# Value products of seven attention heads, one matmul per key block over all queries behind it

## Chip, cores and metric

The kernel runs on one core of one Trainium2 chip. The metric is the device time of one execution in microseconds (us); lower is better. PE is TensorE (PEld its weight loads), DVE is VectorE, ACT is ScalarE, POOL is GpSimd, SP is the engine whose queue issues the loads.

## The reference

One layer of a decoder with 512 tokens and width 1024 in float32. The part that matters here is the attention: two causal mixers with eight heads each, whose outputs are gated and added.

```python
def nsa_mixer(q, kc, vc, ks, vs, kw, vw, gates):
    ...
        s = jnp.einsum('bqgrd,bngd->bgrqn', qb, kc) * scale
        p_cmp = masked_softmax(s, cmp_end[None, :] <= t[:, None])
        o_cmp = jnp.einsum('bgrqn,bngd->bqgrd', p_cmp.astype(vc.dtype), vc)
    ...
        o_slc = jnp.einsum('bgrqkl,bgqkld->bqgrd', p.astype(vs.dtype), v_sel)
    ...
        o_win = jnp.einsum('bgrqk,bkgd->bqgrd', p.astype(vw.dtype), v_w)
        o = gb[..., 0:1] * o_cmp + gb[..., 1:2] * o_slc + gb[..., 2:3] * o_win
def mla_mixer(q, k, v):
    ...
        p = masked_softmax(s, kpos[None, :] <= t[:, None])
        o = jnp.einsum('bhqk,bkhd->bqhd', p.astype(v.dtype), v)
```

With 512 tokens the selected and the window branch both see all keys up to the query, so each is plain causal attention, as the MLA mixer is. What is computed here is, for each head and branch, O = P V with a causal P of 512 queries by 512 keys.

## The kernel before

**Stages.** Norm, adaLN and the first projections (to about 70 us in the trace), key/value group 0 of the NSA mixer together with the compression MLP (to 136 us), the heads (to 545 us), output projection (to 600 us) and the FFN. A matmul on float32 data is made in three: each operand is split into a rounded high part and a low rest (`split`, lines 82 to 84: ACT makes the high part, DVE the rest), and `mm3` (lines 91 to 94) issues high x high, high x low, low x high into one PSUM group.

**Weights.** `load_w` (lines 99 to 116) takes a raw tile `wr` from a pool of five (`raw_unit`, line 97), loads 128 x 512 floats into it from SP's queue, and splits it into `wh` and `wl` (four tiles of each). The raw tile is free when DVE has made `wl`. The same pool serves the adaLN products (`gemv`, lines 124 to 128) and, in `kv_group`, the two rope tables (lines 241 to 244), which stay in their raw tiles until `rope_2x2` (lines 207 to 216) has run for both token halves. In the stage to 136 us a round of the group's `gemm256` (lines 186 to 200) splits one tile of key or value weights for 24 matmuls of 256 columns and then lets the compression take four tiles, each for four matmuls of 256 columns.

**Heads.** `half` (lines 734 to 786) does 256 queries of one head and branch: scores, softmax, transposes of the probabilities by PE, `split` into `PTh` and `PTl`, and then the value products in `pv` (lines 721 to 732). The probabilities' transposes lie key block by key block, each for the queries that see it. Half 0 has queries 0 to 255 and key blocks 0 and 1, half 1 has queries 256 to 511 and key blocks 0 to 3. So the products are `mm3` groups of

```python
                if j <= a:
                    o, r = O[:, c0:c0 + 256], slice(j * 256, (j + 1) * 256)
                else:
                    o, r = O[:, c0 + P:c0 + 256], slice((a + 1) * 256, (a + 1) * 256 + P)
                mm3(o, vh, vl, PTh[:, r], PTl[:, r], first and j == 0, j == a + 1)
```

256 columns, and of 128 for the last key block of the half. An NSA head has two such branches (`nsa_half`, lines 814 to 827) and the compressed one (`cmp_lane`, lines 788 to 812); an MLA head has one (`mla_half`). Heads 0 to 6 go through `nsa_head` and `mla_head` (lines 838 to 849), head 7 is written out by halves.

**Order.** The tile framework's scheduler makes the order on each engine at build time, from priorities and from which tiles are free; each engine then runs its list in order. `pv` has a raised priority. So a change in a pool's size or in one helper moves instructions elsewhere.

Of the kernel before, what the change touches and what calls it, by code (L numbers as in the profile page):

```python
# [10 lines left out]
F32 = mybir.dt.float32  # L11
F32R = mybir.dt.float32r
# [5 lines left out]
P = 128  # L18
# [20 lines left out]
def tile_hybrid_layer(  # L39
# [56 lines left out]
    def raw_unit():  # L96
        return wp.tile([P, 512], F32, name="wr", tag="wr", bufs=5)
# [39 lines left out]
    # ---------------------------------------------------------------- constants  # L137
# [38 lines left out]
    krp = const.tile([P, NT, 2, RD], F32, name="krp")  # L176
# [8 lines left out]
    # ================================================================ heads  # L185
# [181 lines left out]
    def mla_kv(h):  # L367
# [26 lines left out]
        vec.tensor_mul(kraw, kraw, rk.unsqueeze(2).to_broadcast([P, NT, HD]))  # L394
        vec.tensor_tensor(krp, krr.unsqueeze(2).to_broadcast([P, NT, 2, RD]),
# [12 lines left out]
    # ================================================================ phase 1  # L408
    with tc.tile_pool(name="p1", bufs=1) as p1:
# [126 lines left out]
        # ---- cq and the branch gates  # L536
# [17 lines left out]
        # ---- second group: ckv, kr, vc of the second group  # L554
# [12 lines left out]
        # ---- compressed branch inputs, features on partitions  # L567
# [16 lines left out]
        # ---- ckv, kr  # L584
# [31 lines left out]
        # gains and constants of the heads  # L616
# [8 lines left out]
        # ---- compression  # L625
# [79 lines left out]
    # ================================================================ attention  # L705
# [3 lines left out]
    with tc.tile_pool(name="p2", bufs=1) as p2:  # L709
# [24 lines left out]
        def half(hf, qk, V, nrq, gate, O, first, sc=None):  # L734
# [37 lines left out]
            blocks = []  # L772
            for j in range(a + 2):
                for x2 in range(2):
                    if j <= a + x2:
                        blocks.append(off[x2] + j * P)
            PTh = p2.tile([P, 896], F32R, name="PTh", tag="PTh", bufs=2)
            PTl = p2.tile([P, 896], F32R, name="PTl", tag="PTl", bufs=2)
            for b0 in range(0, len(blocks), 4):
                bl = blocks[b0:b0 + 4]  # L780
                tr = bank("T")
                for e, o in enumerate(bl):
                    pe.transpose(tr[:, e * P:(e + 1) * P], Pt[:, o:o + P], ident)  # L783
                cs = slice(b0 * P, (b0 + len(bl)) * P)
                split(PTh[:, cs], PTl[:, cs], tr[:, 0:len(bl) * P])
            pv(O, first, hf, (PTh, PTl), V)

        def cmp_lane(h, sc, O, i0, i1):
# [20 lines left out]
            pt = p2.tile([P, 896], F32R, name="pt", tag="PTh", bufs=2)[0:96, 0:n * P]  # L809
# [4 lines left out]
        def nsa_half(h, hf, O, sc):  # L814
            qh, ql, _, nrq = NQ[h]
            Kt, V = KV[h // 4]
            for br in range(2):
                kh, kl = Kt[br]

                def vf(j, br=br):  # L820
                    s = slice((j % 2) * 256 + br * P, (j % 2) * 256 + (br + 1) * P)
                    return V[j // 2][0][:, s], V[j // 2][1][:, s]
                qf = [lambda ts, q=q: q[:, ts] for q in (qh, ql)]
                half(hf, [(qf[0], kh), (qf[0], kl), (qf[1], kh)], vf, nrq, gates[:, 3 * h + 1 + br, :], O, hf == 0 and br == 0,
                     None if br else sc)
                if not br and (hf or h == 7):
                    cmp_lane(h, sc, O, 2 * hf if h == 7 else 0, 2 * hf + 2)

        def mla_half(h, hf, O):
# [5 lines left out]
            half(hf, [(qn[0], knh), (qn[0], knl), (qn[1], knh), (qr[0], krh), (qr[1], krl[0:RD])],  # L835
                 lambda j: (vh[:, j * P:(j + 1) * P], vl[:, j * P:(j + 1) * P]), nrq[:, h % 2, :], None, O, hf == 0)

        def nsa_head(h):
            O = bank("O")
            sc = sm.tile([P, NT, 32], F32, name="sc", tag="sc", bufs=1)  # L840
            nsa_half(h, 0, O, sc)
            nsa_half(h, 1, O, sc)
            return O

        def mla_head(h):
            O = bank("O")
            mla_half(h, 0, O)
            mla_half(h, 1, O)
            return O
# [22 lines left out]
        for h in range(7):  # L872
# [11 lines left out]
            if h < 6:  # L884
                acc = p2.tile([P, 512], F32, name="acc2", tag="acc2")
                if h < 4:
                    c0, dst = ((3 * D, fS), (4 * D, fA))[h // 2]
                    c0 += (h % 2) * 512
                    gemv(acc, c0, True)
                    gemv_cols(acc, c0, dst[:, 4 * (h % 2):4 * (h % 2) + 4], h >= 2)  # L890
                else:
                    gate_acc(acc, 2 * D, h - 4)
                    gate_out(ga, acc, h - 4)
# [13 lines left out]
    # ================================================================ output projection and FFN  # L907
# [214 lines left out]
```

## Time and profile before

| | us |
|---|---|
| median of 3 runs | 950.85 |
| lowest, highest | 950.5, 951.32 |
| span of the profiled execution | 947.3 |
| PE matmul busy | 914.3 |
| DVE busy | 690.8 |
| ACT busy | 511.0 |

The span is the time between the first and the last instruction in the profile; the runs' times hold about 3.5 us more, for what lies around it (the profiled execution has no time of its own beside its span). Busy PE is a modelled figure, since matmuls overlap: a matmul's own duration says little, the step from one start to the next is its price. In the tables a line of `kernel.py` is L and its number; L87 is the one line that issues all of `mm`'s matmuls, so they are told apart by their operands (`psO<-PTh,Vh` is a value product of the NSA mixer, `psO<-PTh,vh` one of the MLA mixer).

### The profile page before, as it was taken

The page shows a single profiled execution, that of the slowest core. Times are in us where ns is not written, and L with a number is a line of the kernel's source. Part 1 is how long each engine was busy: PE and PEld are TensorE (multiplying, and loading weights), DVE is VectorE, ACT ScalarE, POOL GpSimd, SP SyncE. Part 2 cuts the span into 40 slices and gives each one's busy share as a digit, 9 for nine tenths or more (in the row PEclk, how much of TensorE's full clock was granted, in tenths as well). Part 3 has the DMA queues.
Part 4 walks back from the last instruction along what each step waited for, and adds up shares of the span by engine and source line. Part 5 has one row for each costly group of instructions (what it writes and reads, how often), then busy time and mean ns, then how long its engine had stood idle before and what let it go on. Part 6 is the DMA issues. An engine that isn't in the chain of part 4 may idle for free.

```text
span 947.3 us, 15181 instructions
## 1 busy us (share of the span) xinstructions
PE 914.3 (97%) x5271; PEld 801.2 (85%) x5271; DVE 690.8 (73%) x1513; ACT 511.0 (54%) x1241; POOL 51.1 (5%) x57
## 2 busy tenths in 40 slices
PE   3999899999999999999999999999999999999998
PEld 2899788889889998888889899988888888888886
DVE  6967979787977779688967788797787666622423
ACT  5556758566676557558766655445444444422221
POOL 1000101001000001001001010000000000000000
PEclk9999999999999999999999999999999999999999
DMA  9945682441331253341214265263363333333421
GB/s 298 341 112 145 180 232 82 134 136 35 115 87 34 57 170 101 101 128 43 56 46 134 75 189 150 76 175 107 95 183 101 93 97 100 94 96 101 143 91 44
DMA packets 135778, 113.06 MB, mean 119 GB/s; under 512 B 7514, under 2 KB 118678, under 8 KB 135702
## 3 DMA queue, kind: packets, MB, share of 16 engines
q1 hardware_dynamic: 134934, 110.00, 39.4%
q0 software_dynamic: 768, 2.11, 0.7%
q8 instruction: 41, 0.67, 0.3%
q14 instruction: 35, 0.29, 0.1%
HBM read 109.98 MB, written 2.10 MB: 118 GB/s over the span
## 4 chain that ended last, share of the span: by engine, by line
PE 87%; ACT 4%; DVE 4%; DMA 3%; issue 1%; SPq 0%; POOL 0%; DVEq 0%; ACTq 0%
PE psG L87 43%; PE psS L87 23%; PE psO L87 8%; PE psF L87 4%; PE psT L87 4%; PE psT L783 2%; DMA wr<-in_w_in_dram 1%; DVE wl L84 1%; ACT Pt L760 1%; DMA wr<-in_cmp_v_w_dram 1%; ACT wh L83 1%; DMA ada<-in_w_ada_dram 1%; DMA x<-in_x_dram 1%; ACT sq L223 1%; PE psT L808 0%
## 5 line engine op out<-in xcount | busy, mean ns | idle before, releaser
L83 ACT ACTIVATE wh<-wr 128x512 fp32r<-128x512 f32 (+3 forms) x304 | 186.7, 621 | 289.5 <-PE psS L87 95.0
L84 DVE TENSOR_TENSOR wl<-wr,wh 128x512 fp32r<-128x512 f32 (+3 forms) x304 | 203.6, 676 | 155.4 <-ACT wh L83 148.4
L87 PE MATMUL psG<-hTh,wh 128*128 128x512 f32 x192 | 76.5, 398 | 1.0 <-DVE qr L328 1.0
L87 PE MATMUL psG<-hTh,wl 128*128 128x512 f32 x192 | 76.3, 397 | 0.1
L87 PE MATMUL psG<-hTl,wh 128*128 128x512 f32 x192 | 76.3, 397 | 0.0
L87 PE MATMUL psS<-h2l,wh 128*128 128x512 f32 (+1 forms) x184 | 68.3, 371 | 0.0
L87 PE MATMUL psS<-h2h,wl 128*128 128x512 f32 (+1 forms) x184 | 68.2, 371 | 0.0
L87 PE MATMUL psG<-h2h,wh 128*128 128x512 f32 (+1 forms) x184 | 68.2, 372 | 0.0
L87 PE MATMUL psG<-h2h,wl 128*128 128x512 f32 (+1 forms) x184 | 68.2, 371 | 0.0
L87 PE MATMUL psG<-h2l,wh 128*128 128x512 f32 (+1 forms) x184 | 68.1, 371 | 0.0
L87 PE MATMUL psS<-h2h,wh 128*128 128x512 f32 (+1 forms) x184 | 68.0, 370 | 0.0
L760 ACT ACTIVATE Pt<-psS,nm 128x128 f32<-128x128 f32 (+2 forms) x96 | 51.1, 534 | 25.8 <-DVE nm L755 20.1
L83 ACT ACTIVATE PTh<-psT 128x384 fp32r<-128x384 f32 (+1 forms) x72 | 36.5, 528 | 22.4 <-PE psT L783 22.2
L84 DVE TENSOR_TENSOR PTl<-psT,PTh 128x384 fp32r<-128x384 f32 (+1 forms) x72 | 42.1, 597 | 8.7 <-ACT PTh L83 8.1
L122 DVE SCALAR_TENSOR_TENSOR acc<-wr,csil,acc 128x512 f32<-128x512 f32 x60 | 44.8, 747 | 2.7 <-DMA wr<-in_w_ada_dram 1.5
L87 PEld LDWEIGHTS psG<-hTh,wh 128*128 128x128 f32 x192 | 36.2, 188 | 7.6 <-PE psS L87 0.7
L87 PEld LDWEIGHTS psG<-hTh,wl 128*128 128x128 f32 x192 | 36.1, 188 | 7.1 <-DVE wl L84 0.5
L87 PEld LDWEIGHTS psG<-hTl,wh 128*128 128x128 f32 x192 | 36.1, 188 | 6.4
L87 PE MATMUL psG<-wh,hTh 128*128 128x256 f32 (+2 forms) x128 | 37.5, 303 | 2.5 <-ACT hTh L83 1.4
L87 PEld LDWEIGHTS psG<-h2h,wl 128*128 128x128 f32 x184 | 34.7, 189 | 6.0
L87 PEld LDWEIGHTS psS<-h2l,wh 128*128 128x128 f32 x184 | 34.7, 189 | 6.0
L87 PEld LDWEIGHTS psS<-h2h,wh 128*128 128x128 f32 x184 | 34.7, 188 | 6.0
(431 smaller groups left out, 2593.8 us busy)
## 6 DMA issues: line engine op xcount, KB each, us to landing
wr<-in_w_up_dram SPq DMA_DIRECT2D x88, 256.0 KB, 3.0
wr<-in_w_ada_dram SPq DMA_DIRECT2D x64, 256.0 KB, 2.9
wr<-in_w_in_dram SPq DMA_DIRECT2D x48, 256.0 KB, 3.0
wr<-in_w_down_dram SPq DMA_DIRECT2D x44, 256.0 KB, 2.6
ada<-in_w_ada_dram SPq DMA_DIRECT2D x32, 256.0 KB, 5.4
wr<-in_w_o_dram SPq DMA_DIRECT2D x32, 256.0 KB, 3.0
wr<-in_w_in_dram SPq DMA_DIRECT2D x32, 128.0 KB, 3.6
wr<-in_cmp_k_w_dram SPq DMA_DIRECT2D x16, 256.0 KB, 3.7
```

Source lines behind the costliest of these rows:

```text
L83: act.activation(hi, src, AF.Copy)
L84: vec.tensor_sub(lo, src, f(hi))
L87: ins = pe.matmul(o, lhsT, rhs, start=start, stop=stop, skip_group_check=True)
L122: vec.scalar_tensor_tensor(acc, w, csil[:, k:k + 1], acc, op0=ALU.mult, op1=ALU.add)
L223: act.activation(sq[:, 0:n], b, AF.Square, accum_out=dst)
L760: act.activation(Pt[:, off[x2]:off[x2] + nt[x2]], Sb[x2], AF.Exp, bias=nm[:, x2:x2 + 1], scale=-1.0, accum_out=sums[:, x2:x2 + 1])
L783: pe.transpose(tr[:, e * P:(e + 1) * P], Pt[:, o:o + P], ident)
```

## The change

For heads 0 to 6 the probabilities of both halves of a branch go into one pair of tiles, and `pv_head` issues the products when both are there: key block j meets all queries from block j on, in one `mm3` group of 512, 384, 256 and 128 columns. For key block 0 the columns lie in two pieces (0 to 255 and 640 to 895), which one access pattern reads. The tiles `PTh`, `PTl` and `pt` grow from 896 to 1280 columns, two of each as before. In turn the pool `wr` has four tiles in place of five, `krp` moves from a tile of its own into the tag `kr` (which `c2` of `comb_b` also uses), and `acc2` into a tile of the tag `U`. `cmp_lane` runs once per head for all four query blocks, as it did for these heads. Head 7 keeps its halves.

```diff
     def raw_unit():
-        return wp.tile([P, 512], F32, name="wr", tag="wr", bufs=5)
+        return wp.tile([P, 512], F32, name="wr", tag="wr", bufs=4)
...
-    krp = const.tile([P, NT, 2, RD], F32, name="krp")
...
+        krp = pj.tile([P, 512], F32, name="krp", tag="kr").rearrange("p (t a d) -> p t a d", t=NT, a=2)
...
+        HEAD_BLOCKS = (((0, 0), (0, 1), (1, 1)), ((1, 2), (1, 3), (0, 2), (0, 3), (2, 2), (2, 3), (3, 3)))
+        HEAD_AT = {1: (256, 384), 2: (896, 256), 3: (1152, 128)}
+
+        @priority(lambda: 100)
+        def pv_head(O, first, PT, V):
+            for j in range(NT):
+                vh, vl = V(j)
+                if j == 0:
+                    ph, pl = (bass.AP(tensor=t.tensor, offset=t.offset, ap=[t.ap[0], [640, 2], [1, 256]]) for t in PT)
+                else:
+                    at, n = HEAD_AT[j]
+                    ph, pl = (t[:, at:at + n] for t in PT)
+                mm3(O[:, j * P:S], vh, vl, ph, pl, first and j == 0, j == NT - 1)
...
-            PTh = p2.tile([P, 896], F32R, name="PTh", tag="PTh", bufs=2)
-            PTl = p2.tile([P, 896], F32R, name="PTl", tag="PTl", bufs=2)
+            if PT is None:
+                order = [(j, a + x2) for j in range(a + 2) for x2 in range(2) if j <= a + x2]
+                PTh = p2.tile([P, 1280], F32R, name="PTh", tag="PTh", bufs=2)
+                PTl = p2.tile([P, 1280], F32R, name="PTl", tag="PTl", bufs=2)
+                to = 0
+            else:
+                order = HEAD_BLOCKS[hf]
+                PTh, PTl = PT
+                to = hf * 384
...
+            if PT is not None:
+                return
             pv(O, first, hf, (PTh, PTl), V)
...
         def nsa_head(h):
             O = bank("O")
             sc = sm.tile([P, NT, 32], F32, name="sc", tag="sc", bufs=1)
-            nsa_half(h, 0, O, sc)
-            nsa_half(h, 1, O, sc)
+            for br in range(2):
+                args = nsa_args(h, br)
+                PT = pair_of_pt()
+                for hf in range(2):
+                    half(hf, *args, O, False, None if br else sc, PT)
+                pv_head(O, br == 0, PT, args[1])
+                if not br:
+                    cmp_lane(h, sc, O, 0, NT)
             return O
...
         def mla_head(h):
             O = bank("O")
-            mla_half(h, 0, O)
-            mla_half(h, 1, O)
+            PT = pair_of_pt()
+            for hf in range(2):
+                args = mla_args(h, hf)
+                half(hf, *args, O, False, None, PT)
+            pv_head(O, True, PT, args[1])
             return O
...
-                acc = p2.tile([P, 512], F32, name="acc2", tag="acc2")
+                acc = slot("U", "acc2")
```

PE, value products of half 0 of one NSA branch, before (`Vh` and `Vl` are the value block's high and low parts):

```order
L87 MATMUL psO<-PTh,Vh_1737 128x256
L87 MATMUL psO<-PTl,Vh_1737 128x256
L87 MATMUL psO<-PTh,Vl_1738 128x256
L87 MATMUL psO<-PTh,Vh_1737 128x128
L87 MATMUL psO<-PTl,Vh_1737 128x128
L87 MATMUL psO<-PTh,Vl_1738 128x128
```

Half 1 of the branch has, at another place of the list, nine more of 256 columns and three of 128.

PE, value products of a whole NSA branch, now, from its first matmul to its last:

```order
L87 MATMUL psO<-PTh,Vh_1736 128x512
...
L87 MATMUL psO<-PTl,Vh_1736 128x512
L87 MATMUL psO<-PTh,Vl_1737 128x512
L87 MATMUL psO<-PTh,Vh_1736 128x384
L87 MATMUL psO<-PTl,Vh_1736 128x384
L87 MATMUL psO<-PTh,Vl_1737 128x384
L87 MATMUL psO<-PTh,Vh_1740 128x256
L87 MATMUL psO<-PTl,Vh_1740 128x256
L87 MATMUL psO<-PTh,Vl_1741 128x256
L87 MATMUL psO<-PTh,Vh_1740 128x128
L87 MATMUL psO<-PTl,Vh_1740 128x128
L87 MATMUL psO<-PTh,Vl_1741 128x128
```

Eighteen matmuls in two places have become twelve in one; four projection matmuls stand where the line of dots is.

DVE, the rope of key group 0, first token half, before (`kg` is the key with its gain, the two rows with `wr` read the rope tables, each `wl` frees a weight's raw tile):

```order
L204 TENSOR_TENSOR kg<-psS,rowg 128x512
L84 TENSOR_TENSOR ckvTl_1053<-psF,ckvTh_1052 128x512
L208 TENSOR_TENSOR a_1389<-kg,wr 128x512
L84 TENSOR_TENSOR wl<-wr,wh 128x512
L211 TENSOR_TENSOR a_1390<-kg,wr 128x512
L84 TENSOR_TENSOR wl<-wr,wh 128x512
```

And now:

```order
L203 TENSOR_TENSOR kg<-psS,rowg 128x512
L84 TENSOR_TENSOR ckvTl_1052<-psF,ckvTh_1051 128x512
L207 TENSOR_TENSOR a_1388<-kg,wr 128x512
L210 TENSOR_TENSOR a_1389<-kg,wr 128x512
L84 TENSOR_TENSOR wl<-wr,wh 128x512
```

The reads of the tables have moved ahead of weight splits: from this `kg` to the last read of a table, for the second token half, five `wl` stood before and three stand now. SP's list of loads is the same in this stage in both.

## Rows read from the trace of the kernel before

**Rows 1.** The page's first part: busy us (share of the span) and instructions.
```profile
PE 914.3 (97%) x5271; PEld 801.2 (85%) x5271; DVE 690.8 (73%) x1513; ACT 511.0 (54%) x1241; POOL 51.1 (5%) x57
```

**Rows 2.** Busy time by stages, with the columns' names.
```profile
core 0: us, PE busy (x) PEld busy (x) DVE busy (x) ACT busy (x) POOL busy (x), PEclk, DMA share, GB/s
...
100.00:136.00 36.00, 32.36 (x235) 28.69 (x235) 30.87 (x58) 25.44 (x61) 5.27 (x3) 1.00 0.73 211
...
150.00:545.00 395.00, 387.70 (x2471) 344.85 (x2471) 318.49 (x832) 258.39 (x755) 31.67 (x29) 1.00 0.32 91
...
600.00:947.00 347.00, 342.95 (x1541) 284.90 (x1539) 209.27 (x314) 131.93 (x214) 0.55 (x1) 1.00 0.36 109
```

**Rows 3.** Waits, 100 to 136 us: us in total, times, longest.
```profile
SPq L112 <- DVE wl L84: 13.1, 11, 2.0
...
ACT wh L83 <- DMA wr<-in_cmp_v_w_dram: 3.0, 3, 2.0
PEld psG L87 <- DVE wl L84: 1.8, 3, 0.9
```

**Rows 4.** The chain in order of time: start, us, what.
```profile
148.94 1.56 PE psG L87 x9
...
542.44 18.64 PE psG L87 x155
...
653.86 5.44 PE psS L87 x24
```

**Rows 5.** Timeline of PE, value products: start, us, engine, line, operands.
```profile
266.61 0.33 PE L87 MATMUL psO<-PTh,Vh 128*128 128x256 f32 x1
266.78 0.28 PE L87 MATMUL psO<-PTl,Vh 128*128 128x256 f32 x1
...
267.30 0.44 PE L87 MATMUL psG<-hTh,wl 128*128 128x512 f32 x1
...
508.74 0.28 PE L87 MATMUL psO<-PTl,vh 128*128 128x256 f32 x1
...
509.69 0.22 PE L87 MATMUL psO<-PTh,vh 128*128 128x128 f32 x1
509.75 0.28 PE L87 MATMUL psO<-PTl,vh 128*128 128x128 f32 x1
509.87 0.27 PE L87 MATMUL psO<-PTh,vl 128*128 128x128 f32 x1
509.98 0.62 PE L403 MATMUL psF<-ident,krp 128*128 128x128 f32 x4
```

**Rows 6.** DMA issues, 100 to 136 us: count, KB each, us to landing.
```profile
wr<-in_cmp_v_w_dram SPq DMA_DIRECT2D x16, 256.0 KB, 3.0
```

**Rows 7.** Groups of instructions, 85 to 136 us: busy, mean ns, idle before.
```profile
L83 ACT ACTIVATE wh<-wr 128x512 fp32r<-128x512 f32 x39 | 23.8, 631 | 9.6 <-DMA wr<-in_cmp_v_w_dram 3.0 <-PE psO L87 1.6 <-DMA wr<-in_w_in_dram 1.5
...
L84 DVE TENSOR_TENSOR wl<-wr,wh 128x512 fp32r<-128x512 f32 x39 | 26.1, 685 | 3.7 <-ACT wh L83 3.6
```

**Rows 8.** Timeline of SP's queue, 101 to 131 us (issues in a row are merged).
```profile
101.48 0.34 SPq L243 DMA_DIRECT2D wr<-in_rope_c_dram  x1
102.22 0.34 SPq L243 DMA_DIRECT2D wr<-in_rope_s_dram  x1
103.42 0.89 SPq L112 DMA_DIRECT2D wr<-in_w_in_dram  x2
...
113.18 0.88 SPq L112 DMA_DIRECT2D wr<-in_w_in_dram  x2
...
118.23 1.15 SPq L112 DMA_DIRECT2D wr<-in_w_in_dram  x2
...
124.08 0.88 SPq L112 DMA_DIRECT2D wr<-in_w_in_dram  x2
...
130.01 1.09 SPq L112 DMA_DIRECT2D wr<-in_w_in_dram  x2
```

**Rows 9.** Timeline of DVE, the last read of a rope table.
```profile
116.91 0.68 DVE L211 TENSOR_TENSOR a<-kg,wr 128x512 f32<-128x512 f32 x1
```

More of the change, by code (lines that the diff above doesn't have):

```diff
@@ L732, in pv, with half @@
                 mm3(o, vh, vl, PTh[:, r], PTl[:, r], first and j == 0, j == a + 1)
-        def half(hf, qk, V, nrq, gate, O, first, sc=None):
+        HEAD_BLOCKS = (((0, 0), (0, 1), (1, 1)), ((1, 2), (1, 3), (0, 2), (0, 3), (2, 2), (2, 3), (3, 3)))
[10 more added lines that the diff above has]
+                mm3(O[:, j * P:S], vh, vl, ph, pl, first and j == 0, j == NT - 1)
+        def half(hf, qk, V, nrq, gate, O, first, sc=None, PT=None):
             a = 2 * hf
@@ L771, in half @@
                     vec.tensor_scalar(v, v, r[:, x2:x2 + 1], None, op0=ALU.mult)
[L772 to L776, printed above, removed]
-            PTh = p2.tile([P, 896], F32R, name="PTh", tag="PTh", bufs=2)
-            PTl = p2.tile([P, 896], F32R, name="PTl", tag="PTl", bufs=2)
+            if PT is None:
[7 more added lines that the diff above has]
+                to = hf * 384
+            blocks = [off[i - a] + j * P for j, i in order]
             for b0 in range(0, len(blocks), 4):
@@ L783, in half @@
                     pe.transpose(tr[:, e * P:(e + 1) * P], Pt[:, o:o + P], ident)
-                cs = slice(b0 * P, (b0 + len(bl)) * P)
+                cs = slice(to + b0 * P, to + (b0 + len(bl)) * P)
                 split(PTh[:, cs], PTl[:, cs], tr[:, 0:len(bl) * P])
+            if PT is not None:
+                return
             pv(O, first, hf, (PTh, PTl), V)
@@ L808, in cmp_lane @@
                 pe.transpose(tr[0:96, i * P:(i + 1) * P], p3[:, i].rearrange("p a n -> p (a n)"), ident)
-            pt = p2.tile([P, 896], F32R, name="pt", tag="PTh", bufs=2)[0:96, 0:n * P]
+            pt = p2.tile([P, 1280], F32R, name="pt", tag="PTh", bufs=2)[0:96, 0:n * P]
             act.activation(pt, tr[0:96, 0:n * P], AF.Copy)
@@ L812, in cmp_lane, with pair_of_pt, nsa_args, vf @@
             mm(O[:, i0 * P:i1 * P], vc3[:, g, :], pt, False, True)
-        def nsa_half(h, hf, O, sc):
+        def pair_of_pt():
+            return [p2.tile([P, 1280], F32R, name=n, tag=n, bufs=2) for n in ("PTh", "PTl")]
+        def nsa_args(h, br):
             qh, ql, _, nrq = NQ[h]
             Kt, V = KV[h // 4]
-            for br in range(2):
[L818 to L829, printed above, removed]
+            kh, kl = Kt[br]
+            def vf(j):
+                s = slice((j % 2) * 256 + br * P, (j % 2) * 256 + (br + 1) * P)
+                return V[j // 2][0][:, s], V[j // 2][1][:, s]
+            qf = [lambda ts, q=q: q[:, ts] for q in (qh, ql)]
+            return [(qf[0], kh), (qf[0], kl), (qf[1], kh)], vf, nrq, gates[:, 3 * h + 1 + br, :]
+        def nsa_half(h, hf, O, sc):
+            for br in range(2):
+                half(hf, *nsa_args(h, br), O, hf == 0 and br == 0, None if br else sc)
+                if not br:
+                    cmp_lane(h, sc, O, 2 * hf, 2 * hf + 2)
+        def mla_args(h, hf):
             qnh, qnl, qst, nrq = MQ[h // 2]
@@ L834, in mla_half @@
             qr = [lambda ts, r=r: qst[hf][r, g * 256 + ts.start % 256:g * 256 + ts.start % 256 + P] for r in (slice(0, P), slice(0, RD))]
-            half(hf, [(qn[0], knh), (qn[0], knl), (qn[1], knh), (qr[0], krh), (qr[1], krl[0:RD])],
-                 lambda j: (vh[:, j * P:(j + 1) * P], vl[:, j * P:(j + 1) * P]), nrq[:, h % 2, :], None, O, hf == 0)
+            return ([(qn[0], knh), (qn[0], knl), (qn[1], knh), (qr[0], krh), (qr[1], krl[0:RD])],
+                    lambda j: (vh[:, j * P:(j + 1) * P], vl[:, j * P:(j + 1) * P]), nrq[:, h % 2, :], None)
+        def mla_half(h, hf, O):
+            half(hf, *mla_args(h, hf), O, hf == 0)
         def nsa_head(h):
@@ L840, in nsa_head @@
             sc = sm.tile([P, NT, 32], F32, name="sc", tag="sc", bufs=1)
-            nsa_half(h, 0, O, sc)
-            nsa_half(h, 1, O, sc)
+            for br in range(2):
[4 more added lines that the diff above has]
+                pv_head(O, br == 0, PT, args[1])
+                if not br:
+                    cmp_lane(h, sc, O, 0, NT)
             return O
```

## Prediction

> **What bounds the kernel now.** I read the page's first two parts first [rows 1]: TensorE's matmuls are busy for 914.3 us of the 947.3 us span, the next engine, VectorE, for 690.8. Then the table by stages [rows 2]: from 150 to 545 us (attention) PE is busy 387.70 of 395 us, from 600 us (the FFN) it is busy all through to the last products, and the granted clock is 1.00, the 2.4 GHz level, in every stage shown. So in attention a nanosecond of PE work that goes is very nearly a nanosecond of the end, and there is little idle time on PE (7.3 us) to win or lose. One stage differs. From 100 to 136 us, where the first key/value group and the compression are built, PE is busy only 32.36 of 36 us, and this is the stage whose weight traffic is heaviest (211 GB/s against 91 in attention). There the waits [rows 3] say who is late: the DMA queue's issues wait for VectorE's `wl` (13.1 us, 11 times: a raw weight tile is free only when `wl` has been made from it), ScalarE's `wh` waits for the DMA (3.0 us), PE's weight loads wait for `wl` (1.8 us). That is a ring: tile free, load, `wh`, `wl`, tile free. The number of `wr` tiles is its length. So two places matter: the price of a matmul in attention, and this ring.
>
> **Part 1: the narrower matmuls that go.** Per head and branch the old code issues 6 + 12 matmuls (half 0: three of 256 columns and three of 128; half 1: nine of 256 and three of 128), the new code 12 (three each of 512, 384, 256, 128). Both stream 3 x 1280 = 3,840 columns, so nothing is won unless a matmul has a price besides its columns. The steps between starts show that it has. In the chain of waits [rows 4] 155 matmuls of 256 columns take 18.64 us, 0.1203 us each; 24 of 512 take 5.44 us, 0.2267 each; nine of 384 take 1.56 us, 0.1733 each. 256 columns more cost 0.2267 - 0.1203 = 0.1064 us, so a matmul costs about 14 ns beside its columns, whatever its width. A group of three with 128 columns takes 0.29 us (509.69 to 509.98), 0.06 + 0.12 + 0.11, far more than the 0.16 us of its columns by that step [rows 5].
> Old price: half 0 took 0.69 us (266.61 to 267.30, six matmuls), half 1 0.12 us for its first and 1.24 us for the other eleven (508.74 to 509.98) [rows 5]; together 2.05 us. New price: 3 x 0.2267 + 3 x 0.1733 + 3 x 0.1203 + 0.29 = 1.85 us. The change is in three branches (two NSA, one MLA) of seven heads, 21 times: 21 x 0.20 = 4.2 us. The first matmul of a group can take longer after a change of width (0.17 us at 266.61); if each of the new group's first matmuls paid 0.05 us of that, the gain would be 3.1 us. I take **-3.8 us**, nearer the upper end, since in the old order the same switches occur.
> The same step by the skill: the Trainium skill's "TensorE: Matmul & The Clock Gate", section "Wait — 56ns, not 53.3ns?", states that warm back-to-back matmuls start N / 2.4 GHz plus about 2.5 ns apart at any width. By it 126 matmuls fewer would be worth an estimated 0.3 us and not 3.8. The trace disagrees for this kernel's fp32r matmuls (14 ns and not 2.5), so the row decides.
>
> **Part 2: four `wr` tiles in place of five.** The probabilities' tiles grow from 896 to 1280 columns, and `wr` pays for it in memory. In attention and in the FFN the weights are split many microseconds before PE wants them, so a shorter ring is covered there by the four `wh`/`wl` tiles; if that cover went, PE would wait on `wl` as it does at 100 us. In the ring stage there is no cover. One turn of a tile costs 0.34 us of issue [rows 8], 3.0 us to landing [rows 6], 0.63 us of `wh` and 0.69 us of `wl` [rows 7]: 4.7 us. A round is five tiles (one of the key/value weights, four of the compression weights) and gives PE 24 + 16 matmuls of 256 columns, 40 x 0.1203 = 4.8 us. Five tiles can give a round every 4.7 us, just PE's pace; four give one every 5 x 4.7 / 4 = 5.9 us. But the rounds already take 5.85 and 5.93 us (118.23 to 124.08 to 130.01) [rows 8], because ScalarE and VectorE have other work. So a round loses nothing if a tile's turn falls to the bare 4.7 us, and 1.5 us if it stays what five tiles at 5.9 us a round make it, 5.9 us (5 x 5.9 / 4 = 7.4). I take 0.6 us, between the two but nearer the bare turn, as fewer loads share the DMA, for the three rounds from 118 us on: 1.8 us (bounds 0 and 4.5). The three rounds before 102 us have spare time in PE's order: 0.2 us (0 to 1.5).
> The round between is worse. The two rope tables sit in `wr` tiles as well, issued at 101.48 and 102.22 us [rows 8] and last read by VectorE at 116.91 + 0.68 us [rows 9]. Of five tiles three were left, and the next round's first load went out 9.76 us after this one's (103.42, 113.18). Of four tiles two are left: five loads at 4.7 / 2 us are 11.8 us, so +2.0 us (0, if VectorE reads the tables earlier: in the new order three `wl` stand before the last read in place of five; 3.5, at a turn of 5.3 us). PE waits for these tiles, so all of it reaches the end. Sum of the part: **+4.0 us**, bounds 0 and 9.5.
>
> **Part 3: what moves.** PE's order shows the products of a branch as one run behind the transposes of both halves. Softmax, transposes and splits are the same in number, so ScalarE and VectorE do not change. A pair of probability tiles is now held for a whole branch, and `cmp_lane` takes one of the two: the next branch's first split waits for the last product of this one, 12 matmuls in place of 6 behind. PE has key, query and gate projections to put between, as now. `krp` shares a tile with `c2` of `comb_b`, and `acc2` takes a spare `U` tile; both have microseconds of room. The scheduler makes a new order of all of it. PE's idle time in attention is 7.3 us in all [rows 2]; I allow 2 us either way and take 0. `c2` and `krp` add no instruction; no DMA is added.
>
> **Sum.** -3.8 + 4.0 + 0 = +0.2 us: a span of 947.5 us where the profiled one has 947.3. The times lie about 3.5 us above the span (median 950.85, 950.5 to 951.32), so I forecast **951.0 us**. A measurement of this kernel can tell about 0.2% (1.9 us) from no change: the forecast is no difference, with 949.0 to 952.7 us as this case's own range.
>
> **Rivals.**
> - Faster: the ring loses 1.5 us or less, because fewer transfers at a time land sooner and the scheduler, which knows of four tiles, puts the rope reads first. Then -3.8 + 1.0 gives 948.0 us (946.5 to 948.9). For it: rounds of 5.9 us are already no shorter than four bare turns allow. Against it: PE starts on `wl` as soon as it is made in this stage, so any delay goes through.
> - Slower: the ring pays near its upper bounds. Place: the loads from 101 to 136 us; price 7 us (rope round 3.5, rounds 3.5); it decides when a tile's turn stays above 5.3 us with four tiles. -3.8 + 7.0 gives 954.0 us (952.8 to 957). For it: the queue already waits on `wl` 11 times there. Against it: DMA is busy only 0.73 of this stage, so landing should not slow down.
> - The wide matmuls are no cheaper, because only columns count; then the first term is 0 and 950.85 + 4.0 gives 954.9 us. Against it stand the 0.1203 and 0.2267 us of [rows 4]. This is what the page's rule above would make of the change.
>
> **How the numbers follow.** No difference 0.40; the faster rival 0.28; the slower rival 0.25; columns only 0.04; 0.03 for another cause that makes it slower, such as a wait for the probability tiles. So faster 0.28, same 0.40, slower 0.32. The range takes the faster rival whole, and the slower one up to 956.5 us: 946.5 to 956.5 us. Below it would need the whole 4.2 us, no loss in the ring and a luckier order in attention.
>
> **What would show it.** Right: 126 matmuls fewer on PE; a product run of 12 in about 1.85 us; PE's idle time grown by 3 to 5 us between 100 and 140 us, with ScalarE's `wh` waiting longer for `wr`; the start of attention late by that and the end of attention level with before. Wrong: the stage to 136 us no later than before (then the faster rival), later by 6 us or more (the slower one), or a product run of 2.0 us (columns only). If the distance from attention's start to its end shrinks by less than 2 us or by more than 6 us, Part 3's zero was wrong.

## The result: 988.5 us, 4% slower, and the profile after

| | before | after |
|---|---|---|
| median, us | 950.67 | 988.51 |
| lowest, highest | 950.08, 951.32 | 986.9, 990.73 |
| span of the profiled execution | 947.3 | 986.5 |
| first score matmul of head 0 | 148.05 | 156.89 |
| end of the last value product | 542.28 | 581.68 |
| between the two (the heads) | 394.2 | 424.8 |
| from there to the end of the span | 405.0 | 404.8 |

The ratio is 1.0405 (95% interval 1.0388 to 1.0423). The starts in PE's timeline split the 39.2 us between the two spans: 8.8 lie ahead of the heads, 30.6 in the heads, none behind them. The forecast had +4.0 and -3.8 there. The medians differ by 37.8 us. In every run on record a time lies 1.7 to 2.3 us above its own span, so the profiled execution of before took an estimated 949.4 us, 1.3 below the median; the 3.5 us used ahead of the forecast compared a median with the span of another execution.

The page's first part and the clock's line of its second (40 slices), after:

```profile
PE 931.7 (94%) x5145; PEld 806.7 (82%) x5145; DVE 693.4 (70%) x1513; ACT 514.7 (52%) x1241; POOL 47.8 (5%) x57
...
PEclk9999899989999999979999999999999999999999
```

PE has 126 matmuls fewer than in [rows 1], VectorE and ScalarE have as many instructions as there, and yet PE is busy 17 us longer. The clock's line says why: three slices are below 9. The stages, as in [rows 2], and two shorter stretches:

```profile
core 0: us, PE busy (x) PEld busy (x) DVE busy (x) ACT busy (x) POOL busy (x), PEclk, DMA share, GB/s
...
100.00:136.00 36.00, 28.60 (x193) 26.53 (x193) 26.38 (x51) 20.60 (x53) 3.47 (x3) 0.86 0.58 161
...
150.00:545.00 395.00, 372.69 (x2139) 320.69 (x2138) 298.56 (x780) 243.73 (x724) 31.79 (x29) 0.97 0.30 85
...
230.00:250.00 20.00, 20.00 (x115) 17.15 (x114) 12.69 (x29) 9.50 (x22) 1.38 (x1) 1.00 0.01 3
250.00:260.00 10.00, 7.80 (x34) 5.71 (x33) 9.60 (x28) 6.42 (x17) 0.00 (x0) 0.83 0.63 179
```

Between 150 and 545 us PE is idle for 22.3 us where it was idle for 7.3, and the granted clock is 0.97 in place of 1.00. Over the heads alone (156.89 to 581.68 us, and 148.05 to 542.28 before) the idle time is 24.0 us against 7.3 and the busy time 400.8 against 386.9: of the 30.6 us, 16.7 are more waiting and 13.8 are work that takes longer although there is less of it. The last two rows show the pattern of one head: for 20 us the DMA engines move almost nothing (3 GB/s) while PE is still fed, and in the next 10 us PE stands still for 2.2 us and the clock falls. So the loads stop first, and PE runs out of work behind them. In these 10 us VectorE is busy for 9.60.

Which loads? Timeline of VectorE and of SP's queue, the kernel after, second head. SP's merged rows give the time from the first issue to the end of the last; the two rows of `w_ada` at the end are of narrower windows and show the fourth of the eight loads, and the fifth with the sixth. The PE row is its first product of the second head's key weights:

```profile
215.40 38.80 SPq L127 DMA_DIRECT2D wr<-in_w_ada_dram  x8
...
220.28 0.69 DVE L906 TENSOR_TENSOR u<-u,c 128x512 f32<-128x512 f32 x1
...
221.95 0.68 DVE L395 TENSOR_TENSOR krp<-krr,rk 128x512 f32<-128x512 f32 x1
...
248.51 0.69 DVE L901 SCALAR_TENSOR_TENSOR u<-bg,psO 128x512 f32<-128x512 f32 x1 [0.71 <-PE psO L87]
...
249.12 0.48 DVE L120 TENSOR_SCALAR acc<-wr,csil 128x512 f32<-128x512 f32 x1
...
254.97 0.38 SPq L112 DMA_DIRECT2D wr<-in_w_ukv_dram  x1
...
228.04 0.33 SPq L127 DMA_DIRECT2D wr<-in_w_ada_dram  x1
...
249.63 1.67 SPq L127 DMA_DIRECT2D wr<-in_w_ada_dram  x2
...
209.27 0.80 PE L87 MATMUL psG<-wh,ckvTh 128*128 128x256 f32 x2 [0.22 <-ACT wh L83]
```

And the kernel before, first and second head:

```profile
161.30 0.48 DVE L120 TENSOR_SCALAR acc<-wr,csil 128x512 f32<-128x512 f32 x1
...
191.35 0.69 DVE L864 SCALAR_TENSOR_TENSOR u<-bg,psO 128x512 f32<-128x512 f32 x1 [1.18 <-PE psO L87]
...
197.49 0.68 DVE L395 TENSOR_TENSOR krp<-krr,rk 128x512 f32<-128x512 f32 x1
...
213.93 0.68 DVE L869 TENSOR_TENSOR u<-u,c 128x512 f32<-128x512 f32 x1
...
182.20 20.01 SPq L127 DMA_DIRECT2D wr<-in_w_ada_dram  x8
202.76 0.38 SPq L112 DMA_DIRECT2D wr<-in_w_ukv_dram  x1
...
187.02 0.39 PE L87 MATMUL psG<-wh,ckvTh 128*128 128x256 f32 x1
```

Two things are read from these rows. First, `acc` (the tile acc2, the sum of the modulation's weights). Before, its first step ran at 161.30, 30 us ahead of `comb_a`'s `u` at 191.35. After, it runs 0.6 us behind `u` (248.51, 249.12). Of the six heads that have an acc2, five show this lag of 0.6 to 0.7 us, and these five had leads of 30 to 48 us before; the fourth had none (3.5 us behind `u` before, 4.9 after). Both are now tiles of the tag U, `comb_a` stands ahead in the program, and acc2 gets its tile only when `u` has been written. Its weights are loaded all the same: the eight `w_ada` loads begin at 215.40, the fourth is issued at 228.04 and the fifth at 249.63. So four of them fill the four raw tiles and wait there for 249.12, and the next key weights (`w_ukv`), which PE wants, are issued at 254.97, behind the second head's `u`. Before, the same load was issued at 202.76, 42 us ahead of that `u` (244.36). PE shows it as well: its products of the second head's key weights began at 187.02 before, 4.3 us ahead of the first `u`, and begin at 209.27 after, 12.0 us behind it (197.24). Second, `krp`. Before, it was made at 197.49, 16.4 us ahead of the addition that is the last reader of `c` (the tile c2) at 213.93. After, it stands right behind that addition (220.28, 221.95). Both now have the one tile of the tag kr; whether that or the late `w_ukv` holds krp here is asked below.

### The profile page after: what moved, and what is told of

Read it like the earlier page. It is cut to its first block, busy times and chain, and to the rows that moved or that the text cites. A ratio compares the mean times of both kernels' runs of the same rounds, so it can differ in the third digit from the quotient of the medians.

```text
span 986.5 us, 14926 instructions
## 1 busy us (share of the span) xinstructions
PE 931.7 (94%) x5145; PEld 806.7 (82%) x5145; DVE 693.4 (70%) x1513; ACT 514.7 (52%) x1241; POOL 47.8 (5%) x57
## 4 chain that ended last, share of the span: by engine, by line
PE 79%; DVE 8%; DMA 6%; ACT 4%; issue 2%; SPq 0%; POOL 0%; DVEq 0%; ACTq 0%
PE psG L87 39%; PE psS L87 21%; PE psO L87 7%; PE psF L87 4%; PE psT L87 4%; PE psT L801 2%; DMA ada<-in_w_ada_dram 2%; DMA wr<-in_w_in_dram 2%; DMA wr<-in_w_ukv_dram 2%; ACT wh L83 1%; DVE wl L84 1%; DVE acc L122 1%; DMA wr<-in_w_ada_dram 1%; DVE psS L770 1%; DMA x<-in_x_dram 0%
## 5 line engine op out<-in xcount | busy, mean ns | idle before, releaser
L801 PE MATMUL psT<-ident,Pt 128*128 128x128 f32 x240 | 40.1, 292 | 2.2 <-ACT Pt L784 2.0
```

## The experiments

Ratios are to the kernel before, timed on the same chip, with their 95% interval; medians in us. The kernel before took 949.6 to 950.05 there.

The first theories were W (the shorter ring of raw tiles makes weights late in the heads too), O (branch by branch in place of half by half leaves PE without work) and P (a pair of probability tiles held for a whole branch holds up the next one). When none of the three had explained the heads, K (krp waits for c2) and D (products deferred behind both halves cost it) followed, then U (acc2 waits for `u` and holds the ring) with its rival C (only the edits together cost it). The runs stand here by what they tell, not in the order in which they were made: the four of W, O and P first, then krp, the memory edits and the old widths, then acc2, then the rest.

### Single edits put into the kernel before

**Four raw tiles** (`tag="wr", bufs=5` becomes 4):

> The kernel before with four raw weight tiles in place of five, and nothing else. Theory W (the shorter ring of raw tiles makes weights late all through the heads): most of the +37.8 us is here, 975 us or more, with PE waiting for wl and wh between 150 and 560 us. Rival theory O (the heads' new order of halves and branches starves PE) and theory P (a pair of probability tiles held for a whole branch does): only the stage from 100 to 136 us pays, by the prediction's +4.0 us (0 to 9.5): 951 to 960 us, and the attention stage keeps its length.

961.9 us, ratio 1.012 (1.0103 to 1.0137). The first score starts at 156.6, 8.6 us later than before; the heads take 398.8, 4.6 more. Its stage from 100 to 136 us:

```profile
100.00:136.00 36.00, 28.48 (x191) 26.37 (x190) 26.17 (x51) 20.60 (x52) 4.08 (x3) 0.86 0.56 161
```

Idle time and clock are those of the kernel after. So the ring's price ahead of the heads is what that kernel pays there (8.8). Theory W falls for the heads: 4.6 of their 30.6 us come with it.

**Branch by branch** (the loops over half and branch in `nsa_head` exchanged):

```diff
...
-            nsa_half(h, 0, O, sc)
-            nsa_half(h, 1, O, sc)
+            for br in range(2):
+                for hf in range(2):
+                    nsa_branch(h, hf, br, O, sc)
+                if not br:
+                    cmp_lane(h, sc, O, 0, NT)
```

> The kernel before with one thing changed: an NSA head goes branch by branch (half 0, half 1 of the first branch, then of the second) in place of half by half; old matmul widths, old probability tiles of 896 columns per half, five raw tiles. Theory O: two halves of one branch in a row leave the scheduler no other branch's work between scores and value products, so PE idles in attention: 970 to 980 us and cold stretches of the clock. Theories W and P: no change beyond a scheduler's luck, 948 to 954 us.

949.6 us, ratio 0.9996 (0.9987 to 1.0006). Theory O falls: the order of the halves costs nothing in the kernel before.

**krp into kr**, the edit of the diff and no other (`krp = pj.tile(..., tag="kr")` in `mla_kv`):

> The kernel before with krp moved from a tile of its own into the tag kr of c2, and nothing else (five raw tiles, halves). Theory K (the next head's key projection of MLA is made late, because its krp has to wait for c2 of the head before, so PE runs out of filler work in the heads): 970 us or more, with idle time on PE between 160 and 560 us. Theory D (value products deferred until both halves are ready cost it, the memory edits don't): 948 to 953 us.

968.9 us, ratio 1.0203 (1.0187 to 1.0218); the start of the heads is 149.9, the heads take 413.1 with PE idle for 16.7 (7.3 before). Timeline of VectorE, second head:

```profile
215.11 0.69 DVE L869 TENSOR_TENSOR u<-u,c 128x512 f32<-128x512 f32 x1
216.26 0.68 DVE L395 TENSOR_TENSOR krp<-krr,rk 128x512 f32<-128x512 f32 x1
```

The 16 us of lead have become a lag of 1.2 us, from that edit alone. Theory K holds in the kernel before, at a price just under the 970 us that it named.

**acc2 into U**, the edit of the diff and no other (`acc = slot("U", "acc2")`):

> The kernel before with acc2 moved from a tile of its own into the tag U, and nothing else. Theory U (a tag's tiles are given out in the order of first use, so the next modulation's sum cannot start before comb_a has written its tile u; its weights then sit in raw tiles and block the ring): slower by what the memory edits together (991.2) leave after four raw tiles (961.9) and krp (968.9), 991.2 - 950 - 11.9 - 18.9 = 10 us: 960 us, with weights of w_ada lying 20 us and more in their raw tiles. Rival theory C (only the edits together cost it, each tile has spare time alone): 949 to 952 us.

982.6 us, ratio 1.0344 (1.0322 to 1.0365): three times what was expected, and nearly the whole loss from one line. SP's queue and VectorE, second head:

```profile
203.65 38.51 SPq L127 DMA_DIRECT2D wr<-in_w_ada_dram  x8
242.89 0.38 SPq L112 DMA_DIRECT2D wr<-in_w_ukv_dram  x1
...
238.39 0.69 DVE L864 SCALAR_TENSOR_TENSOR u<-bg,psO 128x512 f32<-128x512 f32 x1
239.00 0.48 DVE L120 TENSOR_SCALAR acc<-wr,csil 128x512 f32<-128x512 f32 x1
```

The same picture with five raw tiles and old products: the `w_ada` loads spread over 38.5 us around the wait for `u`, and `w_ukv` comes behind them.

**All edits of memory**, no edit of order or width (the two above, `bufs=4` for `wr`, 1280 columns for `PTh`, `PTl` and `pt`):

> The kernel before with all edits of memory and none of order or width: four raw tiles, krp in kr, acc2 in U, 1280-column probability tiles used in halves. Theory K: 980 to 995 us, the whole loss without one changed product. Theory D: as four raw tiles alone, 958 to 965 us.

991.2 us, ratio 1.0436 (1.0409 to 1.0463), as slow as the changed kernel. So the new products are not needed for the loss. The single edits cost 12, 19 and 33 us, 64 in sum, and 41 together, so they overlap. The trace shows one such overlap: with acc2 alone in U, krp runs behind c2's last reader (212.05, 206.67) although it still has a tile of its own, because its `w_ukv` is issued at 195.64 us (168.92 before).

### Single edits taken from the changed kernel

**Misses first.** Three kernels relieved one tile and became no faster. The edits, one a kernel:

```diff
-            pt = p2.tile([P, 1280], F32R, name="pt", tag="PTh", bufs=2)[0:96, 0:n * P]
+            pt = slot("U", "pt", F32R)[0:96, 0:n * P]
...
-        krp = pj.tile([P, 512], F32, name="krp", tag="kr").rearrange("p (t a d) -> p t a d", t=NT, a=2)
+        krp = slot("U", "krp").rearrange("p (t a d) -> p t a d", t=NT, a=2)
...
-            t2 = pj.tile([P, 512], F32, name="c2", tag="kr")[:, cs]
+            t2 = BG[8 + h][:, cs]
```

> The changed kernel with the compressed branch's probabilities (pt) in a tile of the tag U in place of one of the two PTh tiles, so that the second branch's pair need not wait for the first branch's value products. Nothing else. Theory P: the splits of the second branch can start a branch earlier, the attention stage shrinks by 15 us or more: 955 to 973 us. Theories O and W: 985 to 990 us, as the changed kernel.

> The changed kernel with krp in a tile of the tag U in place of kr, and nothing else. Theory K: most of the loss in the heads goes, 955 to 968 us, near four raw tiles alone (961.9) less the 4 us of the wide matmuls. Theory D: 985 to 992 us.

> The changed kernel with comb_b's c2 written into the tile of its gate (bg) in place of a tile of the tag kr, so that krp has kr for itself in the heads. Nothing else. Theory K: the 19 us of krp alone come back, or less where the ring is blocked anyway: 970 to 980 us. If the earlier miss with krp in U says that krp costs nothing here: 985 to 992 us.

990.6, 997.9 and 1002.5 us, ratios 1.0424, 1.0519 and 1.0545. The first says that the compressed branch's tile is not the cause. The other two seemed to clear krp. They had left acc2 in U, and their traces show that in the second head krp came no earlier for it: at 219.65 and 222.82 where the changed kernel has 221.95, with `w_ukv` issued at 203.38 and 206.55 (205.69). The third head is alike (267.18, 271.55; 269.81); only in the fourth is krp earlier, by 12 us and more (310.82, 314.91; 327.18). So in these first heads krp's wait for c2 was not the one that ended last, and the two runs say little about it. That they are slower by 9 to 14 us, and not just equal, was not settled.

**Both branches' pairs held at once** (`nsa_head` of the changed kernel):

```diff
+            args = [nsa_args(h, br) for br in range(2)]
+            PT = [pair_of_pt() for br in range(2)]
+            for hf in range(2):
+                for br in range(2):
+                    half(hf, *args[br], O, False, None if br else sc, PT[br])
+                    if hf:
+                        pv_head(O, br == 0, PT[br], args[br][1])
...
```

> The changed kernel with the old order of work in an NSA head: half 0 of both branches, then half 1 of both, each branch's wide value products behind its half 1, with two pairs of probability tiles in use at once. Wide matmuls, four raw tiles and 1280-column tiles stay. Theory O: most of the loss in attention goes, 950 to 960 us. Theory W: no change, 985 to 990 us. Theory P: the pairs are held longer still, so the loss stays or grows, 985 to 1000 us.

1001.0 us, ratio 1.0535 (1.052 to 1.0551), 12 us over the changed kernel. Theory O had said the opposite; that holding the pairs longer is what costs the 12 us (P) fits, and was not separated from the order that came with it. (A later run below holds one pair for a whole branch, as the changed kernel does, and loses nothing.)

**Old widths behind both halves** (in `pv_head`, pieces of 256 and 128 columns of the same tiles):

```diff
+                if j == 0:
+                    parts = [(0, 0, 256), (256, 640, 256)]
+                elif j == 1:
+                    parts = [(P, 256, 128), (256, 384, 256)]
+                else:
+                    parts = [(j * P, *HEAD_AT[j])]
...
```

> The changed kernel with its value products in the old widths: per branch 18 matmuls of 256 and 128 columns in place of 12 of 512 to 128, still in one run behind both halves. If a matmul costs 14 ns beside its columns, 21 branches times 0.20 us, +4.2 us against the changed kernel: about 992.5 us. If only columns count: 988.5 us. If long matmuls themselves harm the order or the clock: 980 us or less.

995.1 us, ratio 1.0481 (1.0463 to 1.0498), so the wide matmuls are worth 6.6 us there, with what the new order of that kernel adds or takes.

**acc2 out of U**, into the half of `ga` that is not yet written. One line of the changed kernel:

```diff
-                acc = slot("U", "acc2")
+                acc = ga[:, 512:1024]
```

> The changed kernel with one edit undone: acc2 lies in the second half of the tile ga, which is written only after it has been read, and not in the tag U. krp in kr, four raw tiles and wide products stay. Theory U (acc2 in U is the largest part of the loss, because its weights fill the raw tiles and wait): 965 to 976 us (950 + 19 for krp + 12 for four raw tiles - 5 for the wide products at most). If other edits hide it: 983 us or more.

973.1 us, ratio 1.0243 (1.0226 to 1.026): 15.4 us back. SP's queue and VectorE, second head:

```profile
194.99 19.85 SPq L127 DMA_DIRECT2D wr<-in_w_ada_dram  x8
215.18 0.38 SPq L112 DMA_DIRECT2D wr<-in_w_ukv_dram  x1
...
207.94 0.48 DVE L120 TENSOR_SCALAR ga<-wr,csil 128x512 f32<-128x512 f32 x1
...
250.08 0.68 DVE L901 SCALAR_TENSOR_TENSOR u<-bg,psO 128x512 f32<-128x512 f32 x1
```

The sum starts 42 us ahead of `u` again, and `w_ukv` is issued at 215.18 and not at 254.97.

**The same, and c2 in its gate's tile:**

> The changed kernel with acc2 in the second half of ga and c2 in the tile of its gate; four raw tiles and the two full Pt tiles stay. Against the run with acc2 in a tile of its own and a Pt tile per half (963.3 us): the same within 2 us if the split of Pt costs nothing; 955 to 959 us, the sum of four raw tiles (+12) and the wide products (-4 to -6.6), if the split Pt is what is left of the loss. Against the run with krp still shared (973.1): 10 us less if krp in kr counts once acc2 is out of U.

960.9 us, ratio 1.012 (1.0104 to 1.0135): 12.2 us back. With acc2 out of the way the edit that was a miss counts.

**acc2 in a tile of its own** instead, c2 still in its gate's tile, with the room taken from Pt:

```diff
-            Pt = p2.tile([P, 896], F32, name="Pt", tag="Pt", bufs=2)
+            Pt = p2.tile([P, 384 + 512 * hf], F32, name="Pt", tag=f"Pt{hf}")
```

> The changed kernel with two of its three memory edits undone: c2 in the tile of its gate (krp has kr for itself), acc2 in a tile of its own again; the room comes from Pt, one tile of 384 columns for half 0 and one of 896 for half 1 in place of two of 896. Four raw tiles and the wide products stay. If the three memory edits are the whole loss: 950 + 11.9 (four raw tiles) - 3.8 to -6.6 (wide products) = 955 to 958 us. If the deferred products cost something of their own: 965 us or more.

963.3 us, ratio 1.0147 (1.013 to 1.0164). The split of Pt costs 2.4 us at most.

**Five raw tiles as well**, once with acc2 still in U but with the first step of its sum ahead of `comb_a`, once with acc2 in `ga`; both have c2 in its gate's tile and Pt by halves. The first one's own edit:

```diff
+            if h < 6:
+                acc = slot("U", "acc2")
...
+                    gemv(acc, c0, True, range(1))
...
             comb_a(h, Oa)
...
-                    gemv(acc, c0, True)
+                    gemv(acc, c0, True, range(1, KD))
```

> The changed kernel with five raw tiles again (room from Pt as above), c2 in the tile of its gate, and acc2 still in U but with the first step of its sum written ahead of comb_a, so that its tile is given out first. If the three memory edits are the whole loss and first use decides the order of U: 950 - 3.8 to -6.6 = 943 to 947 us, faster than both. If acc2 in U still blocks the ring: 950 to 960 us.

> The changed kernel with all three memory edits undone and its products kept: acc2 in the second half of ga, c2 in the tile of its gate so that krp has kr for itself, five raw tiles (the room from Pt, 384 columns for half 0 and 896 for half 1). If the memory edits are the whole loss: the gain of the wide products is left, 950 - 3.8 to -6.6 = 943 to 946 us. If products that wait for both halves cost as much as they gain: 948 to 952 us. If they cost more: 953 us and above.

959.7 us, ratio 1.0103 (1.0087 to 1.012), and 957.0 us, 1.0077 (1.0058 to 1.0096). In both the heads take 402 us (402.5, 402.1): used first, a tile of U is as good as one elsewhere, so it was the order of first use that made acc2 wait. The trace of the first one agrees: acc2's first step now stands 0.6 us behind the `u` of the head before its own (192.31 behind 191.71, 244.21 behind 243.61), the tile of U that is first used just ahead of it. The heads start at 149.2 and 147.9, so the ring's price is gone. But neither beats the kernel before, although no memory edit is left that was shown to cost more than the 2.4 us.

**The products by halves again**, in that last kernel and in the old widths (18 matmuls a branch):

```diff
...
                 for hf in range(2):
                     half(hf, *args, O, False, None if br else sc, PT)
-                pv_head(O, br == 0, PT, args[1])
+                    pv_head(O, br == 0 and hf == 0, PT, args[1], hf)
...
```

> The kernel that took 957.0 us (the change with its three memory edits undone) with one thing changed: each half's value products are issued behind that half again, in the old widths (18 matmuls a branch). If the deferral behind both halves costs more than the wide matmuls give: 946 to 952 us. If the rest of that kernel costs it and the products only gain: 957 + 4 to 6.6 = 961 to 964 us.

950.2 us, ratio 1.0002 (0.9993 to 1.0011). So issuing the products behind both halves costs 6.8 us here, with the gain of the wide matmuls already taken off. The pair of probability tiles is held for the whole branch in this kernel too, so what theory P names costs nothing here. One place as an example, the timeline of PE in the first head, products by halves:

```profile
157.35 0.28 PE L87 MATMUL psS<-Kh,qh 128*128 128x256 f32 x1
157.47 0.28 PE L87 MATMUL psO<-PTl,Vh 128*128 128x256 f32 x1
...
160.90 0.50 PE L87 MATMUL psS<-Kh,qh 128*128 128x512 f32 x1 [0.72 <-ACT Pt L771]
```

and behind both halves:

```profile
161.40 0.50 PE L87 MATMUL psO<-PTh,Vh 128*128 128x512 f32 x1 [1.62 <-ACT PTh L83]
162.24 0.50 PE L87 MATMUL psS<-Kh,qh 128*128 128x512 f32 x1 [0.34 <-ACT Pt L775]
...
163.13 0.63 PE L87 MATMUL psG<-hTh,wh 128*128 128x512 f32 x1
163.55 0.63 PE L87 MATMUL psG<-hTl,wh 128*128 128x512 f32 x1
```

In the first, half 0's products stand at 157.47 between the scores, and PE waits 0.72 us. In the second all products stand behind half 1, PE waits 1.62 us for the second half's `PTh`, waits 0.34 again, and at 163.13 us a matmul of 512 columns is followed 0.42 us later and not 0.23: the granted clock is 0.50 from 163 to 166 us.

### Two runs that tried to show the path, or to win

**acc2 in U, and a raw tile of its own for `w_ada` in the heads** (the kernel before otherwise):

```diff
-            w = raw_unit()
+            w = raw_unit() if raw is None else raw()
...
+        def raw_ada():
+            return p2.tile([P, 512], F32, name="wa", tag="wa")
```

> The kernel before with acc2 in the tag U, as in the run that took 982.6 us, and with one raw tile of its own for the loads of w_ada in the heads, so that they cannot fill the ring of the other weights. Theory U by way of the ring: the 33 us go, 948 to 956 us, although acc2 starts as late as before. If acc2's late start costs by another path (VectorE's steps bunched behind comb_a): 970 us or more.

1008.2 us, ratio 1.061 (1.0587 to 1.0632): a miss, and it can't decide what it was made for. `w_ukv` was early again (PE used it at 187.3 us, before `u`), but with one tile for `w_ada` each load waits for the step before, and VectorE, which works in order, waits for the loads. Nor did it last: the fourth head's `w_ukv` stands behind eight such loads in SP's list and was issued at 282.50, where before it was 256.27. Waits of VectorE, 150 to 560 us:

```profile
DVE acc L122 <- DMA wa<-in_w_ada_dram: 35.9, 32, 2.5
```

One stream was unblocked at first, and VectorE blocked in its place. That the raw tiles are the whole path of acc2's 33 us is therefore read from the traces (tiles held, DMA idle, `w_ukv` late) and not isolated by a run. A rival stays open: the eight steps of the sum now come together behind `u`, where VectorE is nearly full (9.60 of 10 us from 250 to 260 us in the kernel after), so part of the price may be VectorE's.

**Six raw tiles in the kernel before**, with the room of acc2 and krp (`bufs=6`; acc2 in `ga`, c2 in its gate's tile, krp in kr):

> The kernel before with acc2 in the second half of ga, c2 in the tile of its gate, krp in kr, and six raw tiles in place of five. If five tiles bind in the stage from 100 to 136 us as four do: 942 to 948 us. If five are enough and the new places cost nothing: 948.5 to 951.5 us. If the places cost: 953 us or more.

959.8 us, ratio 1.0105 (1.0088 to 1.0122). It is slower by 10 us, in the heads (405.7). The places of acc2, c2 and krp cost nothing in the run with products by halves, so the sixth raw tile and the order that the scheduler makes from it are left as the cause, which no run isolates; which wait decides there stays open. Seven raw tiles, the first plan, do not fit into the memory. No version beat the kernel before.

## Why the prediction was wrong

Peeled off the changed kernel one after the other, the parts sum up:

| step | median | start of heads | heads |
|---|---|---|---|
| changed kernel | 988.5 | 156.9 | 424.8 |
| acc2 out of U | 973.1 | 155.7 | 410.1 |
| and krp freed of c2 | 960.9 | 157.1 | 399.4 |
| and five raw tiles (Pt by half) | 957.0 | 147.9 | 402.1 |
| and products by halves | 950.2 | 147.4 | 393.9 |

- **Part 3 failed: "`krp` shares a tile with `c2` of `comb_b`, and `acc2` takes a spare `U` tile; both have microseconds of room" and the zero taken for it, with 2 us either way.** The two cost 15.4 + 12.2 = 27.6 us in this order of peeling. I looked at whether a tile is free for long enough, and not at who must have finished before the next user of the tag gets it. The rows of before had the answer: acc2's first step 30 us ahead of `u`, krp 16 us ahead of c2's last reader. A step that runs that far ahead of its new neighbour can only be late behind it.
- **The same part said that PE "has key, query and gate projections to put between".** Those need weights, and the weights need raw tiles. With the ring held by `w_ada`, this cover ran out (DMA busy for 0.01 from 230 to 250 us, PE idle for 2.2 of the next 10). The deferral costs something even with the ring free: 6.8 us net with five raw tiles. With four it can't be seen: 960.9 against 961.9 us for the kernel before with four. So its size belongs to the order that is made around it.
- **Part 2, +4.0 us with bounds 0 and 9.5, was right in place and sign and low in size.** 8.6 us in the run with four tiles alone. SP's queue, the kernel after, shows where it was mis-sized:

```profile
107.13 0.89 SPq L112 DMA_DIRECT2D wr<-in_w_in_dram  x2
...
121.58 0.88 SPq L112 DMA_DIRECT2D wr<-in_w_in_dram  x2
...
139.45 1.73 SPq L112 DMA_DIRECT2D wr<-in_w_in_dram  x2
```

The first of these loads is 3.7 us later than before (103.42 in [rows 8]), where 0.2 was allowed for the rounds ahead of it, 1.5 at most. The round with the rope tables takes 14.45 us and not 9.76: +4.7, where +2.0 was worked out and 3.5 was the bound. The three rounds behind take 17.87 us (121.58 to 139.45) where 16.83 stood (113.18 to 130.01 in [rows 8]): +1.0, where +1.8 was worked out. Between 100 and 136 us the granted clock fell to 0.86 as well, which no bound of mine had as a term; (1 - 0.86) x 36 is 5.0 us of clock, an upper bound of what it cost, since PE also waited in these stretches.
- **Part 1, -3.8 us, was right in sign.** An unbroken run of the new kernel:

```profile
246.34 0.50 PE L87 MATMUL psO<-PTh,Vh 128*128 128x512 f32 x1
246.68 0.39 PE L87 MATMUL psO<-PTl,Vh 128*128 128x512 f32 x1
246.91 0.40 PE L87 MATMUL psO<-PTh,Vl 128*128 128x512 f32 x1
247.14 0.34 PE L87 MATMUL psO<-PTh,Vh 128*128 128x384 f32 x1
...
248.31 0.39 PE L87 MATMUL psS<-knh,qnh 128*128 128x384 f32 x1
```

It takes 1.97 us where 1.85 was worked out: the first step is 0.34 us and not 0.23, the others are as forecast. Against the 2.05 us of [rows 5] that is 0.08 us, 1.7 us over 21 branches; the run with old widths says 6.6. Between these the size stays open (the run with old widths also has a lower mean clock, 0.975 against 0.980).
- **Of the rivals** the slower one named a mechanism that did come (the ring), with 954 us. None named a tile that is handed over too late (0.03 was left for other causes), so the range ended 32 us below the result.

## What to carry to other kernels

Where an edit puts a tile into a tag that others use, look in the trace of before for the step that first writes it and for the last reader of the tile that it will follow: if the first runs ahead of the second, the lead is what the edit takes away, and everything behind that step goes with it. A stream that nobody hurries for must not hold the buffers of one that feeds the busiest engine. Undo edits one at a time but also in sums: here one that was worth 12 us looked 14 us harmful until a larger one was gone.

## What was not expected of the hardware

Small waits can cost twice. Before, the granted clock is 1.00 in every stage shown; after, it falls to its lower level (0.50, 1.2 GHz) seven times between 100 and 500 us, for 3.5 to 10.5 us each, and PE's own work then takes longer. Six of these stretches begin behind waits of PE for ScalarE or VectorE, 1.6 to 2.7 us in sum. PE in the second head, after:

```profile
252.89 0.40 PE L87 MATMUL psS<-Kh,qh 128*128 128x288 f32 x1 [0.95 <-ACT Pt L775]
...
254.63 1.94 PE L801 MATMUL psT<-ident,Pt 128*128 128x128 f32 x7 [1.08 <-ACT Pt L784]
256.22 0.69 PE L87 MATMUL psS<-Kh,qh 128*128 128x416 f32 x1
256.71 0.55 PE L87 MATMUL psS<-Kl,qh 128*128 128x416 f32 x1
257.06 0.55 PE L87 MATMUL psS<-Kh,ql 128*128 128x416 f32 x1
257.41 0.63 PE L87 MATMUL psS<-Kh,qh 128*128 128x512 f32 x1
257.83 0.45 PE L87 MATMUL psS<-Kl,qh 128*128 128x512 f32 x1
...
420.00 1.05 PE L87 MATMUL psF<-onesr,sqT 128*128 128x1 f32 x8 [0.20 <-DVE qst L358]
```

Two waits of about a microsecond, and then 416 columns take 0.35 us a step and 512 take 0.42, where 512 take 0.23 at the full clock [rows 4]. The last row belongs to the seventh stretch, and the longest: from 421.5 to 432 us the clock is at its lower level although PE had waited for no more than 0.20 us in the 10 us before. What it did there was eight matmuls of one column in 1.05 us; what made the clock fall is not shown. From 150 to 545 us the mean granted clock is 0.97, which is (1 - 0.97) x 395, about 12 us; PE's added idle time there is 15 us. The Trainium skill's "TensorE: Matmul & The Clock Gate", section "HAM oscillation — how this bites in real kernels", tells of this for a kernel that waits for its loads between tiles: the clock falls in the wait and the next tile starts at 1.2 GHz. This case's trace agrees in six of the seven stretches, here with waits for ScalarE and VectorE.
